# A two-layer attention trunk on one core: each pair of heads handed to the next block inside the last output-projection tile

## The chip, the cores and the metric

The kernel runs on one core of one Trainium2 chip, in fp32 throughout. The metric is device time of one execution in microseconds, here the median of three runs. The engines are named as the profile names them: PE (TensorE matmul), DVE (VectorE), ACT (ScalarE), POOL (GpSimd) and SP (SyncE, which issues nearly every DMA of this kernel).

## The reference

The input is x, 2048 tokens by 1024. Two layers follow one another, each with a residual:

```python
# layer 0
proj = rms_norm(x) @ w_in
ya = sliding_window_sink_attention(aq, ak, av, sinks) * silu(ag)   # 8 query heads of 64
yb = chunked_relbias_attention(bq, bk, bv, rel) * silu(bg)         # 8 heads of 64
x = x + concat(ya, yb) @ w_out
# layer 1
q, k, v, gate = split(rms_norm(x) @ w_in)
a = softmax(q1 k1') - lam * softmax(q2 k2')                        # 8 heads, chunk-causal
o = rms_norm(a v) * (1 - lambda_init)
x = x + (o * silu(gate)) @ w_out
```

The product with w_out is the output projection that this case is about. Its contraction runs over 1024 columns, which are eight groups of 128: in layer 0 a group is a pair of heads of 64, in layer 1 it is one head (whose value width is 128).

## The kernel before

**Precision.** A product that must keep fp32 quality is made of three matmuls of split operands (`mm3`, L212 to L216): high times high, low times high, high times low. The split itself is two instructions: ACT copies the value to the high part, rounded, and POOL subtracts it from the original to give the low part. In layer 0 this is `split_y` (ACT L608, POOL L609, tiles yH and yL), in layer 1 `split` (ACT L997, POOL L998, both tiles called cy).

**Tiling.** The 2048 tokens are four blocks of 512 (`NB`, `BLK`), each of four rows of 128 (`NTB`). The output projection of a block is eight tiles of 128 tokens by 512 columns. A tile takes `KT` = 8 steps, one for each group of 128 contracted columns, of three matmuls each, and ends in an add of the residual on DVE (L501, L1077) and a store. In layer 0 the tiles of a block are done by `projected` through `out_tile`, in layer 1 by `projected` through `out_begin`, `out_step` and `out_end`. A residual tile of layer 1 (xr) and the tiles that hold a fetched head share one pool tag, "ot", with four buffers. The split y of layer 1 takes 16 buffers, which one block fills, so a head of the next block gets its pair only when the last tile of the block before has read that head.

**Two streams, woven.** In both layers `pace` draws from a stream of attention work (`heads`, and behind it the values of each head, lagging by LAG0 or LAG1 units) and a side stream. The side stream's units are the steps of gates and output projections. `pace` lets the side advance to `share(u)`, where u is the attention work done in units; a step that yields 1 counts, whether it issues matmuls or not. In layer 0 the share is 0.85 u; in layer 1 it runs on straight lines through `STAGES1`, of which the last goes from 84 side units at u = 44 to 520 at u = 1088, which is the end of the attention work. Layer 1's side has 4 x 8 x 9 = 288 units of gates, 3 x 8 x 9 = 216 of output tiles of blocks 0 to 2, and 16 of fetches. Side matmuls carry `issue_after(self.anchor)`: they are queued on PE behind the latest score matmul. A scheduler then sets the final order on each engine; each engine runs its own queue in order.

**Between two blocks.** In layer 0 the next block's eight `split_y` are eight side units of their own ahead of its first tile. `heads` also forces the side on (`next(side)`, not counted) when the y tiles of two blocks would not fit. In layer 1 finished heads mostly wait in DRAM (`s["o"]`). `fetch(b)` reads them back one by one (DMA L1008, tile coy) and splits them, one side unit each. Block 0's heads and five of block 3's are split in place and never fetched.

**Attention of layer 1.** For each row of 128 queries, the scores (PE L898, L899) go into four PSUM banks; DVE takes the maximum (L902), ACT the exponential (L905). At the end of a row DVE joins the chunks' sums (L914 to L917: L914 multiplies two 128x8 SBUF tiles). POOL then scales both maps (L921, L930) and adds them (L931); every fifth chunk DVE makes that addition itself (L928). Later PE transposes the probabilities (L944), ACT or DVE copies them out of PSUM (L947, L949), and PE multiplies by the values (L951). At the end of a head POOL multiplies by the gate (L972).

Of the kernel before, what the change touches and what calls it, by code (L numbers as in the profile page):

```python
# [85 lines left out]
class Trunk:  # L86
# [3 lines left out]
    FIN = 18  # L90
    COMB = 5
    BANKS1, LAG1 = (4, 2, 1, 1), (30, 30, 36, 36)
    STAGES1 = ((0, 0), (44, 84), (1088, 520))

    def __init__(self, ctx, tc, args, out):
        self.ctx, self.tc, self.nc = ctx, tc, tc.nc
# [389 lines left out]

    def out_tile(self, y, w, j, t, c, xin, xout, sb, pmm, n, tag, xtag="xr", xbufs=None):
        nc = self.nc  # L490
        tok, cs = slice(t * P, (t + 1) * P), slice(c * 512, (c + 1) * 512)
        xr = sb.tile([P, 512], F32, tag=xtag, name=n + "xr", bufs=xbufs)
        nc.sync.dma_start(xr, xin[tok, cs])
        ps = pmm.tile([P, 512], F32, tag=tag, name=n + "om")
        for k in range(KT):
            self.mm3(
                ps, y[k][0][:, j * P:(j + 1) * P], y[k][1][:, j * P:(j + 1) * P],
                w[0][k][c], w[1][k][c], k == 0, k == KT - 1, self.anchor,
            )
            yield 1  # L500
        nc.vector.tensor_tensor(xr, ps, xr, ALU.add)  # L501
        nc.sync.dma_start(xout[tok, cs], xr)
        yield 1
# [16 lines left out]
    def _mix0(self, es):  # L520
# [84 lines left out]
        def split_y(yt):  # L605
            yH = yp.tile([P, BLK], F32R, tag="yH", name=n + "yH")
            yL = yp.tile([P, BLK], F32R, tag="yL", name=n + "yL")
            nc.scalar.activation(yH, yt, AF.Copy)  # L608
            nc.gpsimd.tensor_tensor(yL, yt, f32(yH), ALU.subtract)  # L609
            return yH, yL  # L610
# [134 lines left out]
                ys[4 + h // 2] = finish(yt, 512 + (h // 2) * P, b)  # L745

        units = [(j, c) for c in range(2) for j in range(NTB)]
        split = [[] for _ in range(NB)]

        def projected(b):  # L750
            for k in range(KT):
                split[b].append(split_y(done[b][k]))
                yield 1
            for j, c in units:
                while next_load(c):
                    pass
                pm, tag = (pO, "O") if b == 0 and j % 2 else (pmm, "om")
                yield from self.out_tile(split[b], w, j, b * NTB + j, c, a["x"], self.x1, yp, pm, n, tag, xbufs=2)

        def late_gate(b, c, wg, h, r0):  # L760
            cs = slice(c * P, (c + 1) * P)
# [80 lines left out]
    def _mix1(self, es):  # L842
# [155 lines left out]
            nc.gpsimd.tensor_tensor(yL, o, f32(yH), ALU.subtract)  # L998
            y[b][h] = yH, yL

        def fetch(b):

            for h in range(8):
                while (h, b) not in ended:
                    yield 0
                if h not in y[b]:
                    o = ot.tile([P, BLK], F32, tag="ot", name=n + "oy")
                    nc.sync.dma_start(o, s["o"][h * P:(h + 1) * P, b * BLK:(b + 1) * BLK])  # L1008
                    split(h, b, o)
                    yield 1  # L1010

        def load_k(h, i, m):

# [66 lines left out]
        def projected(b):  # L1080

            halves = (1, 0) if b % 2 else (0, 1)
            w = [(room[0][:, k, :], room[1][:, k, :]) for k in range(KT)]
            for i, c in enumerate(halves):
                for j in range(NTB):
                    xr, ps, to = out_begin(b, j, c)
                    for k in range(KT):
                        out_step(b, j, k, ps, w)
                        if i == 0 and j == NTB - 1:
                            load_w(halves[1], k, w[k])  # L1090
                        yield 1
                    out_end(xr, ps, to)
                    yield 1
# [72 lines left out]
        def side():  # L1166
            yield from gates()
            for b in range(NB):
                yield from fetch(b)
                yield from projected(b) if b < NB - 1 else projected_last()  # L1170

        def share(u):
# [47 lines left out]
```

## Time and profile before

| what | value |
| --- | --- |
| median of three runs | 2870.75 us (2856.9 to 2872.15) |
| the profiled execution's own time | 2868.88 us |
| its span, first to last instruction | 2867.1 us |
| mean granted TensorE clock | 0.982 |
| PE busy | 2717.2 us |
| DVE busy | 1856.3 us |
| POOL busy | 1595.3 us |
| ACT busy | 1544.8 us |

The profile is of one execution. In a timeline row the first number is the start in microseconds from the start of the span, the second the duration of the merged instructions, then engine, source line, operation, `out<-in`, and the count; brackets give the idle time of the engine ahead of it and what ended it. In a row of windows each engine's busy time in that stretch is given in the order PE, PEld (weight load), DVE, ACT, POOL, then the granted TensorE clock as a share of full speed, the DMA engines' busy share and GB/s.

### The profile page before, as it was taken

What the parts mean: (1) busy time and instruction counts of PE and PEld (TensorE: products, weight loads), DVE (VectorE), ACT (ScalarE), POOL (GpSimd) and SP (SyncE); (2) the same over time, 40 slices, a digit from 0 to 9 for tenths busy, and PEclk for the clock granted to TensorE, in tenths of its full rate; (3) what the DMA queues carried; (4) which work ended last, traced back from release to release, by engine and by line L of the source; (5) the groups of instructions that cost most, each with busy time, mean ns of one, the idle gap of its engine ahead of it and who ended that gap; (6) DMA issues with size and microseconds to landing.
All of it is one profiled execution on the core that took longest, in us unless ns stands there. A gap on an engine that the chain in (4) does not pass through costs nothing.

```text
span 2867.1 us, 43943 instructions
## 1 busy us (share of the span) xinstructions
PE 2717.2 (95%) x13384; PEld 2177.3 (76%) x13384; DVE 1856.3 (65%) x4643; ACT 1544.8 (54%) x4015; POOL 1595.3 (56%) x1740
## 2 busy tenths in 40 slices
PE   7999999998899999899999998999999999899999
PEld 5888888787788888777788887776667777566666
DVE  7752285357788875598708860477777677766761
ACT  4443543367767665343344331577777776656652
POOL 3541251334545354267745650578878787878772
PEclk9999999999999999999999999999999999999999
DMA  5673343738877664567875443887858667354543
GB/s 160 226 239 140 114 142 116 232 107 226 229 188 194 181 180 144 191 219 238 264 245 170 132 145 104 268 244 202 235 171 232 180 199 206 112 171 141 149 137 108
DMA packets 356092, 521.68 MB, mean 182 GB/s; under 512 B 44816, under 2 KB 139792, under 8 KB 355856
## 3 DMA queue, kind: packets, MB, share of 16 engines
q1 hardware_dynamic: 355856, 518.87, 60.5%
q8 instruction: 107, 1.75, 0.3%
q14 instruction: 129, 1.06, 0.1%
HBM read 361.70 MB, written 157.02 MB: 181 GB/s over the span
## 4 chain that ended last, share of the span: by engine, by line
PE 71%; DVE 8%; DMA 7%; ACT 4%; issue 2%; POOL 2%; SPq 1%; DVEq 0%; ACTq 0%; POOLq 0%
PE cO L951 7%; PE p1mm L216 5%; PE p1mm L215 5%; PE p1mm L214 5%; PE cS L898 4%; PE cS L899 4%; PE ctr L944 3%; PE p0mm L214 2%; PE p0mm L216 2%; PE p0mm L215 2%; PE com L214 2%; PE com L215 2%; PE com L216 2%; PE mom L214 2%; PE mom L215 2%
## 5 line engine op out<-in xcount | busy, mean ns | idle before, releaser
L905 ACT ACTIVATE cP<-cS,cnm 128x512 f32<-128x512 f32 (+3 forms) x640 | 397.6, 628 | 191.5 <-DVE cnm L902 170.8
L902 DVE TENSOR_REDUCE cnm<-cS 128x1 f32<-128x512 f32 (+3 forms) x640 | 374.3, 603 | 72.4 <-PE cS L899 65.3
L921 POOL TENSOR_SCALAR cP<-cP,crl,ce 128x512 f32<-128x512 f32 (+3 forms) x288 | 215.8, 762 | 186.9 <-DVE crl L916 99.4
L215 PE MATMUL p1mm<-p1wL,p1hH 128*128 128x512 f32 x768 | 302.3, 394 | 0.4 <-POOL p1wL L310 0.4
L214 PE MATMUL p1mm<-p1wH,p1hH 128*128 128x512 f32 x768 | 301.2, 393 | 0.8 <-ACT p1wH L308 0.8
L216 PE MATMUL p1mm<-p1wH,p1hL 128*128 128x512 f32 x768 | 301.9, 393 | 0.0
L951 PE MATMUL cO<-cpt,cv 128*128 128x512 f32 (+3 forms) x640 | 288.6, 539 | 12.3 <-DVE cpt L949 9.6
L310 POOL TENSOR_TENSOR p0wL<-p0ws,p0wH 128x512 fp32r<-128x512 f32 (+1 forms) x124 | 149.7, 1239 | 265.4 <-ACT p0wH L308 255.8
L931 POOL TENSOR_TENSOR cP<-cP,cP 128x512 f32<-128x512 f32 (+3 forms) x256 | 284.9, 1136 | 1.3
L898 PE MATMUL cS<-ck,cqd 128*128 128x512 f32 (+3 forms) x640 | 263.2, 416 | 18.9 <-ACT cP L905 12.0
L310 POOL TENSOR_TENSOR p1wL<-p1ws,p1wH 128x512 fp32r<-128x512 f32 x128 | 169.7, 1346 | 134.3 <-ACT p1wH L308 128.8
L214 PE MATMUL p0mm<-p0wH,p0hH 128*128 128x512 f32 (+1 forms) x640 | 239.1, 375 | 5.2 <-ACT p0vt L472 3.7
L216 PE MATMUL p0mm<-p0wH,p0hL 128*128 128x512 f32 (+1 forms) x640 | 239.5, 375 | 1.5 <-DVE p0hL L336 1.5
L215 PE MATMUL p0mm<-p0wL,p0hH 128*128 128x512 f32 (+1 forms) x640 | 239.1, 374 | 0.0
L899 PE MATMUL cS<-ck,cql 128*128 128x512 f32 (+3 forms) x640 | 234.0, 370 | 4.0 <-DMA cql<-qL 4.0
L944 PEld LDWEIGHTS ctr<-ident,cP 128*128 128x128 f32 x1088 | 137.6, 142 | 115.0 <-issue 60.9
L930 POOL TENSOR_SCALAR cP<-cP,crl,ce 128x512 f32<-128x512 f32 (+3 forms) x230 | 181.4, 800 | 0.7 <-DVE crl L917 0.7
L944 PE MATMUL ctr<-ident,cP 128*128 128x128 f32 x1088 | 174.7, 275 | 2.8 <-POOL cP L931 2.0
L214 PEld LDWEIGHTS p1mm<-p1wH,p1hH 128*128 128x128 f32 x768 | 144.7, 189 | 29.8 <-ACT p1wH L308 1.0
L215 PEld LDWEIGHTS p1mm<-p1wL,p1hH 128*128 128x128 f32 x768 | 144.7, 188 | 29.6 <-POOL p1wL L310 0.8
L216 PEld LDWEIGHTS p1mm<-p1wH,p1hL 128*128 128x128 f32 x768 | 144.7, 188 | 28.7
L898 PEld LDWEIGHTS cS<-ck,cqd 128*128 128x128 f32 x640 | 123.0, 193 | 49.7 <-ACT cP L905 25.6
(306 smaller groups left out, 7296.2 us busy)
## 6 DMA issues: line engine op xcount, KB each, us to landing
p1ws<-in_od_w_in_dram SPq DMA_DIRECT2D x56, 512.0 KB, 4.4
p0ws<-in_ev_w_in_dram SPq DMA_DIRECT2D x48, 512.0 KB, 4.5
ck<-kH SPq DMA_DIRECT2D x144, 128.0 KB, 3.3
ck<-kL SPq DMA_DIRECT2D x144, 128.0 KB, 3.5
cv<-v SPq DMA_DIRECT2D x72, 256.0 KB, 4.2
cqd<-qH SPq DMA_DIRECT2D x128, 128.0 KB, 4.8
cql<-qL SPq DMA_DIRECT2D x128, 128.0 KB, 4.8
cwH<-wgH SPq DMA_DIRECT2D x64, 256.0 KB, 4.6
```

The costliest lines, as they stand in the source:

```text
L214: mm(ps, aH, bH, start=first, stop=False)
L215: mm(ps, aH, bL, start=False, stop=False)
L216: mm(ps, aL, bH, start=False, stop=last)
L310: low.tensor_tensor(l[:, :width], ws[:, k, :width], f32(h[:, :width]), ALU.subtract)
L898: mm(ps, qd[:, m, js], kt[:, :wd], start=True, stop=False)
L899: self.anchor = mm(ps, ql[:, m, js], kt[:, :wd], start=False, stop=True).ins
L902: nc.vector.tensor_reduce(nm[:, m, z:z + 1], ps, AX.X, ALU.max, negate=True)
L905: nc.scalar.activation(chunks[z][:, :wd], ps, AF.Exp, bias=nm[:, m, z:z + 1], accum_out=acc)
L921: nc.gpsimd.tensor_scalar(p1, p1, rl[:, 0:1], e1, ALU.mult, ALU.mult)
L931: nc.gpsimd.tensor_tensor(p1, p1, p2, ALU.add)
L944: nc.tensor.transpose(tp[:, (j - j0) * P:(j - j0 + 1) * P], us[j][kt // 4][:, kk:kk + P], self.ident)
L951: mm(O[:, j0 * P:], v, T[:, :wd], start=(kt == 0), stop=(kt == nkt - 1), skip_group_check=True)
```

## The change

Layer 0: `out_tile` takes the order of the eight contraction steps and a function that is called behind each step. All tiles now go through the pairs in the order in which they finish (0, 4, 1, 5, 2, 6, 3, 7). In the last tile of blocks 3, 2 and 1, `follow` splits the next block's pair right behind the step that was the last to read that place. `projected` splits only what is still missing, and only such a split yields.

Layer 1: `fetch` handles one head and yields nothing. It is called behind each step of a block's last tile, and once more for what is missing ahead of the block. With the 16 fetch units gone, the end of the last stage goes from 520 to 504.

```diff
-    STAGES1 = ((0, 0), (44, 84), (1088, 520))
+    STAGES1 = ((0, 0), (44, 84), (1088, 504))
...
-        for k in range(KT):
+        for i, k in enumerate(order):
             self.mm3(
                 ps, y[k][0][:, j * P:(j + 1) * P], y[k][1][:, j * P:(j + 1) * P],
-                w[0][k][c], w[1][k][c], k == 0, k == KT - 1, self.anchor,
+                w[0][k][c], w[1][k][c], i == 0, i == KT - 1, self.anchor,
             )
+            if after:
+                after(i)
             yield 1
...
-        split = [[] for _ in range(NB)]
+        split = [{} for _ in range(NB)]
+        ended = [p + 4 * is_b for p in range(4) for is_b in range(2)]
 
         def projected(b):
-            for k in range(KT):
-                split[b].append(split_y(done[b][k]))
-                yield 1
+
+            for k in ended:
+                if k not in split[b]:
+                    split[b][k] = split_y(done[b][k])
+                    yield 1
+
+            def follow(i):
+                k = ended[i]
+                if k in done[b - 1] and len(split[b - 1]) == i:
+                    split[b - 1][k] = split_y(done[b - 1][k])
+
             for j, c in units:
...
+                after = follow if b and (j, c) == units[-1] else None
...
-        def fetch(b):
-
-            for h in range(8):
-                while (h, b) not in ended:
-                    yield 0
-                if h not in y[b]:
-                    o = ot.tile([P, BLK], F32, tag="ot", name=n + "oy")
-                    nc.sync.dma_start(o, s["o"][h * P:(h + 1) * P, b * BLK:(b + 1) * BLK])
-                    split(h, b, o)
-                    yield 1
+        def fetch(h, b):
+
+            if (h, b) in ended and h not in y[b]:
+                o = ot.tile([P, BLK], F32, tag="ot", name=n + "oy")
+                nc.sync.dma_start(o, s["o"][h * P:(h + 1) * P, b * BLK:(b + 1) * BLK])
+                split(h, b, o)
...
                     for k in range(KT):
                         out_step(b, j, k, ps, w)
-                        if i == 0 and j == NTB - 1:
+                        if j == NTB - 1 and i == 0:
                             load_w(halves[1], k, w[k])
+                        elif j == NTB - 1:
+                            fetch(k, b + 1)
                         yield 1
...
             for b in range(NB):
-                yield from fetch(b)
+                for h in range(8):
+                    while (h, b) not in ended and b < NB - 1:
+                        yield 0
+                    fetch(h, b)
                 yield from projected(b) if b < NB - 1 else projected_last()
```

In the changed file the lines of layer 0's mixing stand up to 15 lower, those of layer 1's attention 15 lower (L898 is L913, L931 is L946, L998 is L1013), and L1008 is L1020.

What moves, on PE, at the passage from block 0 to block 1 in layer 1. cS are scores (ck0_29673 and, after, ck0_29642 are the keys of one and the same head, the next one), com an output tile, cy its split head, cO values. Before:

```order
L898 MATMUL cS_30001<-ck0_29673,cqd_29544 128x512
L899 MATMUL cS_30001<-ck0_29673,cql_29545 128x512
L898 MATMUL cS_30021<-ck0_29684,cqd_29544 128x512
L899 MATMUL cS_30021<-ck0_29684,cql_29545 128x512
L214 MATMUL com_29898<-p1hH_18099,cy_29691 128x512
L215 MATMUL com_29898<-p1hL_18100,cy_29691 128x512
L898 MATMUL cS_30027<-ck0_29701,cqd_29544 128x512
L899 MATMUL cS_30027<-ck0_29701,cql_29545 128x512
L898 MATMUL cS_30044<-ck0_29713,cqd_29544 128x256
L899 MATMUL cS_30044<-ck0_29713,cql_29545 128x256
L216 MATMUL com_29898<-p1hH_18099,cy_29692 128x512
```

After, from that head's first score on:

```order
L913 MATMUL cS_29767<-ck0_29642,cqd_29512 128x512
L914 MATMUL cS_29767<-ck0_29642,cql_29513 128x512
L214 MATMUL com_29694<-p1hH_18099,cy_22676 128x512
L215 MATMUL com_29694<-p1hL_18100,cy_22676 128x512
L216 MATMUL com_29694<-p1hH_18099,cy_22677 128x512
L214 MATMUL com_29694<-p1hH_18099,cy_23173 128x512
L215 MATMUL com_29694<-p1hL_18100,cy_23173 128x512
L216 MATMUL com_29694<-p1hH_18099,cy_23174 128x512
L214 MATMUL com_29694<-p1hH_18099,cy_23676 128x512
L966 MATMUL cO_29197<-cpt_29535,cv_29116 128x384
L959 MATMUL ctr_29569<-ident_88,cP0_29111 128x128
L215 MATMUL com_29694<-p1hL_18100,cy_23676 128x512
```

Before, 79 rows without an output step lie ahead of the first com row shown, which belongs to block 1. After, eighteen matmuls of block 0's last tile stand between the first and the second piece of that head's scores (the first eight of them are shown), and block 1's first com row comes 33 rows behind the last.

POOL at the same place: L931 adds two maps, L972 multiplies by the gate, L998 makes the low part of a fetched head. Before:

```order
L972 TENSOR_TENSOR cot<-cot,cgg 128x512
L998 TENSOR_TENSOR cy<-coy,cy 128x512
L931 TENSOR_TENSOR cP_29671<-cP_29671,cP_29722 128x512
L931 TENSOR_TENSOR cP_29682<-cP_29682,cP_29737 128x512
L931 TENSOR_TENSOR cP_29699<-cP_29699,cP_29746 128x512
L998 TENSOR_TENSOR cy<-coy,cy 128x512
L931 TENSOR_TENSOR cP_29711<-cP_29711,cP_29762 128x512
L998 TENSOR_TENSOR cy<-coy,cy 128x512
L921 TENSOR_SCALAR cP_29797<-cP_29797,crl,ce 128x512
```

After:

```order
L946 TENSOR_TENSOR cP_29640<-cP_29640,cP_29687 128x512
L946 TENSOR_TENSOR cP_29651<-cP_29651,cP_29708 128x512
L946 TENSOR_TENSOR cP_29662<-cP_29662,cP_29717 128x512
L946 TENSOR_TENSOR cP_29676<-cP_29676,cP_29727 128x512
L987 TENSOR_TENSOR cot<-cot,cgg 128x512
L1013 TENSOR_TENSOR cy<-coy,cy 128x512 x2
L936 TENSOR_SCALAR cP_29771<-cP_29771,crl,ce 128x512
L1013 TENSOR_TENSOR cy<-coy,cy 128x512
```

Eight operations with two tensor inputs in a row become seven, and the four additions of the maps come ahead of the fetched heads.

SP at the same place: coy is a fetch, cgg a gate, cv values, cxr a residual tile in, out_0_dram a finished tile out. Before, behind three fetches that stand among the next head's query loads:

```order
L964 DMA cgg_30787<-g1_75 128x512
L1008 DMA coy_29808<-o1_76 128x512
L1008 DMA coy_29822<-o1_76 128x512
L1008 DMA coy_29846<-o1_76 128x512
L1024 DMA cv_30269<-v_74 128x4x128
L1008 DMA coy_29860<-o1_76 128x512
L1008 DMA coy_29874<-o1_76 128x512
L1067 DMA cxr_29896<-x1_83 128x512
```

After, behind all of those query loads:

```order
L1020 DMA coy_29698<-o1_76 128x512
L1020 DMA coy_29735<-o1_76 128x512
L1089 DMA out_0_dram<-cxr_29692 128x512
L1020 DMA coy_29785<-o1_76 128x512
L979 DMA cgg_30773<-g1_75 128x512
L1020 DMA coy_29802<-o1_76 128x512
L1020 DMA coy_29829<-o1_76 128x512
L1020 DMA coy_29854<-o1_76 128x512
L1035 DMA cv_30260<-v_74 128x4x128
L1020 DMA coy_29871<-o1_76 128x512
L1020 DMA coy_29888<-o1_76 128x512
L1078 DMA cxr_29923<-x1_83 128x512
```

The fetches no longer stand among the query loads, two of them stand ahead of the last tile's store, and two loads of values and the next keys still stand behind all eight.

More of the change, by code (lines that the diff above doesn't have):

```diff
@@ L757, in projected @@
                 pm, tag = (pO, "O") if b == 0 and j % 2 else (pmm, "om")
-                yield from self.out_tile(split[b], w, j, b * NTB + j, c, a["x"], self.x1, yp, pm, n, tag, xbufs=2)
+                after = follow if b and (j, c) == units[-1] else None
+                yield from self.out_tile(
+                    split[b], w, j, b * NTB + j, c, a["x"], self.x1, yp, pm, n, tag, xbufs=2, order=ended, after=after
+                )
         def late_gate(b, c, wg, h, r0):
```

2 lines of the change are left out of this document (1 added, 1 removed).

## The prediction

> **What bounds the kernel now.** I read the page first, then the busy time in stretches of 50 us, then the timeline of each engine where a stretch falls short.
>
> ```profile
> span 2867.1 us, 43943 instructions
> PE 2717.2 (95%) x13384; PEld 2177.3 (76%) x13384; DVE 1856.3 (65%) x4643; ACT 1544.8 (54%) x4015; POOL 1595.3 (56%) x1740
> ...
> 2250.00:2300.00 50.00, 49.89 (x229) 36.14 (x228) 35.39 (x90) 36.62 (x103) 38.16 (x45) 1.00 0.55 165
> 2450.00:2500.00 50.00, 38.54 (x156) 24.73 (x156) 38.12 (x66) 30.47 (x83) 44.54 (x47) 0.86 0.46 131
> 2650.00:2700.00 50.00, 45.88 (x194) 32.74 (x192) 35.73 (x62) 31.68 (x86) 42.78 (x45) 0.93 0.49 143
> ```
>
> PE is the bound: 150 us of the span are all that it leaves idle. Where side steps are spread evenly (2250 to 2300) nothing is left. The worst stretch of layer 1's attention, 11.5 us idle at a clock of 0.86, is the passage from block 0 to block 1; the passage from block 1 to 2 lies at the head of the last one. On PE at the first:
>
> ```profile
> 2473.57 0.50 PE L214 MATMUL com<-p1hH,cy 128*128 128x512 f32 x1 [0.99 <-ACT cy L997]
> 2477.66 0.50 PE L216 MATMUL com<-p1hH,cy 128*128 128x512 f32 x1 [2.46 <-POOL cy L998]
> 2486.76 2.08 PE L951 MATMUL cO<-cpt,cv 128*128 128x512 f32 x2 [7.18 <-DVE cpt L949]
> ...
> 2485.00:2490.00 5.00, 3.24 (x7) 1.92 (x8) 2.29 (x8) 0.27 (x1) 4.21 (x6) 0.50 0.22 57
> 2490.00:2495.00 5.00, 5.00 (x16) 2.72 (x15) 1.18 (x2) 3.02 (x6) 4.57 (x5) 0.83 0.00 0
> ```
>
> Two waits are for the first fetched head, the third is for DVE. Then the clock costs 3.24 x 0.50 + 5.00 x 0.17 = 2.5 us. The passage loses 0.99 + 2.46 + 7.18 + 2.5 = 13.1 us. What held DVE stands in its own rows and POOL's:
>
> ```profile
> 2468.74 0.16 DVE L916 RECIPROCAL crl<-cl 128x2 f32<-128x2 f32 x1
> 2475.61 9.35 DVE L914 TENSOR_TENSOR cpe<-ce,cla 128x8 f32<-128x8 f32 x1
> 2674.77 0.17 DVE L914 TENSOR_TENSOR cpe<-ce,cla 128x8 f32<-128x8 f32 x1 [0.27 <-ACT ce L913]
> ...
> 2469.10 3.04 POOL L921 TENSOR_SCALAR cP<-cP,crl,ce 128x512 f32<-128x512 f32 x4 [0.75 <-ACT cP L905]
> 2472.11 3.04 POOL L930 TENSOR_SCALAR cP<-cP,crl,ce 128x512 f32<-128x512 f32 x4
> 2475.10 1.28 POOL L972 TENSOR_TENSOR cot<-cot,cgg 128x512 f32<-128x512 f32 x1
> 2483.66 1.28 POOL L998 TENSOR_TENSOR cy<-coy,cy 128x512 fp32r<-128x512 f32 x1
> ```
>
> L914 takes 0.17 us elsewhere. Here it started 0.5 us into POOL's run of eight operations on two tensors (the first and the last of them are shown) and ended when the run did, 9.35 us later. While L914 stood, DVE's copies out of PSUM stood behind it, and PE's value matmuls behind those. The Trainium skill says the same of the cause: "GPSIMD Engine Reference", section Specifications, has GpSimd share its SBUF interfaces with VectorE, with contention for DVE instructions that have two SBUF inputs. It gives no price, and this trace's is the 9.35 us. It speaks against this change, which takes no such operation off POOL; what follows from that is the second rival.
>
> **The change part by part.** No matmul, split or DMA is added or taken away. What goes is eight side units without a matmul at each passage; so eight steps come forward into the time where PE had no side work.
>
> *Layer 1, block 0 to 1.* A run of side steps on PE:
>
> ```profile
> 2836.04 0.39 PE L214 MATMUL com<-p1hH,cyk 128*128 128x512 f32 x1
> 2841.26 0.39 PE L216 MATMUL com<-p1hH,cyk 128*128 128x512 f32 x1
> ```
>
> They are the first and the last of 24, so one costs 5.22 / 23 = 0.227 us and eight steps 5.4 us. POOL starts a row of the attention when DVE's L916 is done (2468.9), spends 6.1 us on eight scalings, and is then on its run; the next L914 came 6.7 us after that L916 and was caught at once. After the change eighteen matmuls of the last tile, 4.1 us, stand inside that row, so L914 comes after some 10.8 us. The run is now seven operations of about 1.23 us and lies from 6.1 to 14.7, so 3.9 us of it are left for L914 to wait out. At PE's share of before (7.18 of 9.35) that leaves 3.0 us idle, a gap like those under 3 us, of which I take no loss of clock. The two waits for the first head I halve to 1.7: it is fetched a tile earlier, but its low part stands at the end of the same POOL run. Gain 13.1 - 4.7 = 8.4 us, between 0 (L914 is caught as before) and 13.1.
>
> *Layer 1, block 1 to 2.*
>
> ```profile
> 2638.19 0.50 PE L898 MATMUL cS<-ck,cqd 128*128 128x512 f32 x1 [0.75 <-ACT cP L905]
> 2641.45 0.39 PE L898 MATMUL cS<-ck,cqd 128*128 128x256 f32 x1 [0.98 <-DVE cnm L902]
> 2642.64 0.50 PE L214 MATMUL com<-p1hH,cy 128*128 128x512 f32 x1 [0.68 <-ACT cy L997]
> 2648.90 0.66 PE L944 MATMUL ctr<-ident,cP 128*128 128x128 f32 x4 [0.65 <-ACT csq L977]
> 2673.33 0.80 PE L898 MATMUL cS<-ck,cqd 128*128 128x512 f32 x1 [3.17 <-ACT cP L905]
> ...
> 2663.93 7.88 DVE L928 SCALAR_TENSOR_TENSOR cP<-cP,cc,cP 128x256 f32<-128x256 f32 x1
> ...
> 2664.07 3.75 POOL L998 TENSOR_TENSOR cy<-coy,cy 128x512 fp32r<-128x512 f32 x3
> 2667.79 3.73 POOL L931 TENSOR_TENSOR cP<-cP,cP 128x512 f32<-128x512 f32 x3
> ...
> 2670.00:2675.00 5.00, 1.83 (x5) 1.38 (x5) 4.62 (x9) 2.50 (x8) 1.52 (x2) 0.76 0.21 70
> 2675.00:2680.00 5.00, 5.00 (x13) 3.32 (x13) 2.63 (x8) 3.13 (x9) 4.46 (x7) 0.55 0.30 92
> ```
>
> Idle 6.2 us, clock 1.83 x 0.24 + 5.00 x 0.45 = 2.7 us, together 8.9. Again a run on POOL, three splits and three additions, held a DVE operation. In the new order POOL has two splits, three additions (one a quarter long) and three splits in a row here, a longer run. So I take half of the first four gaps (1.5) and a quarter of the last with its clock (1.5): 3.0 us, between 0 and 8.9.
>
> *Layer 1, block 2 to 3.* The three fetches now stand in the last tile instead of behind the last head. I cost it at nothing: block 3's first three heads are in place, and their steps cover the fetch; without that cover it would cost the two waits of the first passage, 3.5 us.
>
> *Layer 0.* The order of steps changes no count. Of the passages, block 3 to 2 and block 2 to 1 show losses:
>
> ```profile
> 906.36 0.63 PE L736 MATMUL mtrB<-ident,mPB 128*128 128x128 f32 x4 [0.91 <-DVE mptL L589]
> 908.06 1.12 PE L736 MATMUL mtrB<-ident,mPB 128*128 128x128 f32 x4 [1.07 <-DVE mptL L589]
> 913.66 0.44 PE L736 MATMUL mtrB<-ident,mPB 128*128 128x128 f32 x2 [0.78 <-DVE mptL L589]
> 915.06 0.33 PE L736 MATMUL mtrB<-ident,mPB 128*128 128x128 f32 x1 [0.71 <-DVE mptL L589]
> 1053.63 0.39 PE L582 MATMUL mSB<-mks,mqd 128*128 128x256 f32 x1 [1.57 <-DVE manm L633]
> ...
> 905.00:910.00 5.00, 3.02 (x19) 2.62 (x17) 4.90 (x11) 2.49 (x7) 5.00 (x6) 0.79 1.11 292
> 910.00:915.00 5.00, 3.47 (x20) 2.70 (x18) 3.65 (x10) 4.28 (x14) 3.82 (x7) 0.86 0.99 224
> 1055.00:1060.00 5.00, 5.00 (x23) 4.43 (x22) 2.64 (x12) 3.21 (x13) 1.21 (x3) 0.69 0.25 70
> ```
>
> The first loses 3.5 idle and 3.02 x 0.21 + 3.47 x 0.14 = 1.1 of clock, 4.6 us; the second 1.6 and 5.00 x 0.31 = 1.6, 3.1 us. Counting the yields, `heads` forces the side on by twelve units at one point of the second; after the change it forces none. Eight steps, 5.4 us, fit both holes. I take 3.5 and 2.0, between 0 and 7.7. Block 1 to 0 lies behind the attention, where the order stays but for the splits: nothing.
>
> *What it adds.* First, a block's first tile now follows the last one directly, and its first matmul may wait for DVE to free the only bank:
>
> ```profile
> PE com L214 <- DVE cxr L1077: 5.4, 4, 2.1
> ```
>
> That is 1.35 us a time, 2.7 for two passages (0 to 4.2). Second, layer 1's side runs at 420 instead of 436 units over the same stretch, 3.7% slower. From u = 44 to about 240, where PE isn't yet full, three steps come later: 9 x 0.227 = 2.0 us, of which I take 1.5 (0 to 2.0). Third, ACT's split of a next head waits for the step that last read its place; behind it stand exponentials. PE waited for ACT's fetched split 0.99 us at worst in the rows above, and I count it in the halved waits.
>
> Sum: 8.4 + 3.0 + 3.5 + 2.0 = 16.9; less 2.7 + 1.5 = 4.2; 12.7 us. The profiled execution took 2868.88 us, 1.9 less than the median of 2870.75. 2868.88 - 12.7 gives **2856 us**. One sentence on the clock: "TensorE: Matmul & The Clock Gate" of the Trainium skill, section Why this matters for your kernels, warns of PE gaps over about 3 us, and the trace agrees at 7.18 and 3.17 us.
>
> **The rivals.** *All stalls go.* If no DVE operation meets a POOL run at a passage, all of 13.1 + 8.9 + 7.7 = 29.7 us come back, less 2.0: 2841 us. For it: stretches with even side work have no idle time. Against: the new order still has runs of seven and more.
>
> *The stalls move.* POOL's two-tensor operations are as many as before, and runs of 7, 6 and 8 still stand at the passages. If L914 or L928 is caught as before, layer 1 gains nothing: 2868.9 - 5.5 + 4.2 = 2868 us, no change. For it: the 9.35 and 7.88 us were caught by chance of timing, so others can be.
>
> *SP is held (slower).* A fetch needs one of four "ot" buffers, and the last tile's residual now holds one while the fetches queue:
>
> ```profile
> 2801.95 12.26 SPq L1008 DMA_DIRECT2D coy<-o  x3
> ```
>
> Three fetches held SP for 12.3 us there. In the new order values and the next keys stand behind eight. If SP is held that long at both passages and the loads land 12 us late with 3 us of lead, PE waits 9 us twice and loses 2.5 us of clock twice; with layer 1's gains gone: 2868.9 + 23 - 5.5 + 4.2 = 2891 us. It decides once SP stands longer than the loads' lead. Against: the next head's queries now stand ahead of the fetches, and the passage shown held SP without holding PE.
>
> **How the numbers follow.** My forecast, stalls shortened, has 0.61; all stalls gone 0.11; stalls moved 0.16; SP held 0.12. The measurement can tell 0.5%, 14.4 us, from no change: below 2856.4 is faster. The forecast lies on that line, so half of it (0.31) is faster and half the same. Faster 0.31 + 0.11 = 0.42, same 0.30 + 0.16 = 0.46, slower 0.12. The forecast's own bounds are 2868.9 - 29.7 + 2.0 = 2841 and about 2869. The range leaves out the slow case and a few us more for reordered queues everywhere in layer 1 on both sides: 2836 to 2875.
>
> **What would show it.** Right: side steps on PE through both passages, L914 there under 5 us, idle at the first passage under 6 us, the clock in 50 us there over 0.95. Wrong: a DVE operation of 8 us or more beside a run of POOL (stalls moved), an SP row of fetches over 10 us with PE waiting for ck, cv or cqd (SP held), or new idle time of over 5 us outside the passages, which no term here holds.

## The result, and the profile after

The changed kernel takes 2841.76 us (median of 6 runs, 2832.64 to 2846.43) against 2870.43 us before (6 runs, 2856.9 to 2876.98). The ratio is 0.9901 with a 95% interval of 0.9878 to 0.9923: 28.7 us faster, between 22 and 35. The forecast of 2856 us has the sign right and half of the size; the range of 2836 to 2875 us holds the result.

The page of the changed kernel, span and PE's row:

```profile
span 2841.6 us, 43911 instructions
PE 2707.3 (95%) x13384; PEld 2171.4 (76%) x13384; DVE 1844.8 (65%) x4643; ACT 1543.8 (54%) x4015; POOL 1596.6 (56%) x1740
```

The span is 25.5 us shorter. The work on PE is the same 13384 matmuls, so both executions can be cut at the same points of the work: the bounds are the moments at which 8800, 10600, 11800, 12200 matmuls and so on have started on PE. The busy time in these stretches, of the kernel before and then of the changed one (columns: stretch, its length, then busy time and instructions of PE, PEld, DVE, ACT and POOL, the granted clock, DMA share, GB/s):

```profile
0.00:1793.57 1793.57, 1695.69 (x8800) 1428.80 (x8801) 1135.71 (x2883) 859.13 (x2099) 806.53 (x850) 0.99 0.60 181
1793.57:2207.05 413.48, 393.52 (x1802) 294.30 (x1800) 294.12 (x823) 287.27 (x830) 307.41 (x364) 0.98 0.79 228
2207.05:2471.18 264.13, 261.74 (x1203) 191.72 (x1201) 193.71 (x466) 187.52 (x528) 212.00 (x238) 1.00 0.62 181
2471.18:2580.81 109.63, 95.40 (x400) 66.31 (x401) 73.43 (x135) 62.54 (x168) 85.08 (x93) 0.92 0.51 151
```

```profile
0.00:1792.22 1792.22, 1694.97 (x8800) 1428.92 (x8801) 1138.23 (x2883) 859.85 (x2099) 804.95 (x850) 0.99 0.61 181
1792.22:2194.16 401.94, 387.06 (x1802) 289.42 (x1801) 295.61 (x835) 289.92 (x843) 310.79 (x368) 1.00 0.81 233
2194.16:2459.55 265.39, 263.29 (x1201) 192.28 (x1200) 198.61 (x451) 182.35 (x514) 216.06 (x242) 1.00 0.63 183
2459.55:2554.13 94.58, 92.15 (x402) 65.35 (x401) 63.98 (x145) 65.39 (x177) 81.94 (x87) 0.96 0.56 176
```

Read the lengths against each other. Up to layer 1's attention 1.4 us are gained; in the second row, where the gates are computed and no passage lies, 11.5; then 1.3 are lost; and 15.1 are gained in the row of the first passage. What follows is in the table below: 4.6 us more up to the last stretch, and 5.8 given back there. 1.4 + 11.5 - 1.3 + 15.1 + 4.6 - 5.8 = 25.5 us.

**The first passage.** The timelines of SP, DVE, PE and POOL of the changed kernel there, then its busy time in 5 us:

```profile
2451.24 0.17 DVE L931 RECIPROCAL crl<-cl 128x2 f32<-128x2 f32 x1
2457.11 0.50 SPq L1078 DMA_DIRECT2D cxr<-x  x1
2462.41 0.69 DVE L1088 TENSOR_TENSOR cxr<-com,cxr 128x512 f32<-128x512 f32 x1 [2.27 <-DMA coy<-o]
2463.76 2.07 PE L966 MATMUL cO<-cpt,cv 128*128 128x512 f32 x2 [2.13 <-DVE cpt L964]
2465.69 1.27 POOL L1013 TENSOR_TENSOR cy<-coy,cy 128x512 fp32r<-128x512 f32 x1 [0.66 <-ACT cy L1012]
2467.53 0.17 DVE L929 TENSOR_TENSOR cpe<-ce,cla 128x8 f32<-128x8 f32 x1 [2.32 <-ACT ce L928]
```

```profile
2455.00:2460.00 5.00, 4.54 (x23) 3.07 (x21) 3.58 (x7) 3.31 (x10) 5.00 (x6) 1.00 0.91 179
2460.00:2465.00 5.00, 2.65 (x6) 1.32 (x7) 2.72 (x7) 2.99 (x11) 5.00 (x5) 0.78 0.66 220
2465.00:2470.00 5.00, 5.00 (x11) 2.39 (x10) 0.70 (x5) 2.21 (x7) 2.92 (x4) 0.54 0.66 205
```

The operation that stood 9.35 us on DVE (L914, now L929) takes 0.17 us, and the wait of 7.18 us behind it is gone. It came late enough: 16.3 us behind the row's L931 (L916 before), and 0.6 us after POOL's run of two-tensor operations had ended with the row of L1013 shown. What is left is 2.8 us idle and, with the clock, 2.65 x 0.22 + 5.00 x 0.46 = 2.9 us. It has a new reason: SP issues the last tile's residual, "cxr", only at 2457.1, behind the keys and queries; DVE stands for it at L1088 until 2462.4 (the row names the fetch that SP issued next, which L1088 does not read; the residual landed at 2462.39), its copies out of PSUM stand behind, and PE's value matmuls behind those. The second passage looks alike, in the timelines and in 5 us:

```profile
2617.09 0.69 DVE L1088 TENSOR_TENSOR cxr<-com,cxr 128x512 f32<-128x512 f32 x1 [2.87 <-DMA cxr<-x]
2620.39 1.27 SPq L1020 DMA_DIRECT2D coy<-o  x3
2624.77 0.63 ACT L1012 ACTIVATE cy<-coy 128x512 fp32r<-128x512 f32 x1 [4.09 <-DMA coy<-o]
2625.45 0.50 PE L214 MATMUL com<-p1hH,cy 128*128 128x512 f32 x1 [2.75 <-ACT cy L1012]
```

```profile
2620.00:2625.00 5.00, 2.71 (x14) 1.69 (x13) 3.83 (x10) 0.91 (x3) 4.40 (x6) 1.00 0.67 179
2625.00:2630.00 5.00, 4.54 (x13) 3.28 (x14) 2.35 (x4) 5.00 (x14) 5.00 (x6) 0.66 0.35 115
```

DVE stands 2.87 us for the residual, ACT 4.09 us for a fetched head to land (SP issued it at 2620.39, when the last tile's store had landed at 2620.38 and freed an "ot" buffer), and PE 2.75 us for ACT's split of it: 2.29 + 0.46 us idle and 4.54 x 0.34 = 1.5 us of clock, 4.3 together.

**The end.** PE's timeline behind the last head in the changed kernel, its busy time there, and PE's one wait at that place in the kernel before:

```profile
2806.61 1.12 PE L991 MATMUL cms<-csq,ones 128*128 128x512 f32 x2 [1.35 <-ACT csq L983]
2811.41 0.79 PE L214 MATMUL com<-p1hH,cyk 128*128 128x512 f32 x1 [3.67 <-ACT cyk L1012]
```

```profile
2810.00:2815.00 5.00, 3.59 (x10) 2.89 (x11) 0.69 (x1) 0.63 (x1) 1.28 (x1) 0.66 0.16 52
```

```profile
2826.89 1.13 PE L976 MATMUL cms<-csq,ones 128*128 128x512 f32 x2 [1.35 <-ACT csq L968]
```

Before, side steps were left when the last head was done, and they covered its norm and split. Now they are used up: PE waits 3.67 us more and loses 3.59 x 0.34 = 1.2 us of clock. The change moved work forward out of a place where it was cover.

**The gates' stretch.** Three windows of 10 us in which the kernel before loses and the changed one does not, its timelines in one of them, and the windows of the changed kernel for the same work:

```profile
2110.00:2120.00 10.00, 7.66 (x28) 4.64 (x27) 7.93 (x14) 7.01 (x20) 5.66 (x6) 0.83 0.47 133
2130.00:2140.00 10.00, 6.53 (x30) 4.94 (x28) 8.64 (x13) 4.60 (x16) 8.70 (x10) 1.00 0.72 224
2140.00:2150.00 10.00, 9.84 (x35) 7.20 (x36) 6.15 (x19) 6.98 (x20) 5.60 (x9) 0.83 0.41 122
```

```profile
2133.11 5.12 DVE L914 TENSOR_TENSOR cpe<-ce,cla 128x6 f32<-128x6 f32 x1
2139.22 0.50 PE L898 MATMUL cS<-ck,cqd 128*128 128x512 f32 x1 [3.43 <-ACT cP L905]
```

```profile
2110.00:2120.00 10.00, 10.00 (x51) 7.98 (x50) 7.49 (x20) 7.26 (x22) 10.00 (x12) 1.00 0.85 197
2120.00:2130.00 10.00, 9.70 (x42) 6.74 (x41) 9.04 (x23) 7.37 (x25) 8.44 (x10) 1.00 0.81 256
2130.00:2140.00 10.00, 10.00 (x48) 7.22 (x47) 9.34 (x17) 7.73 (x20) 9.38 (x12) 1.00 0.34 102
```

From 2110 to 2150 the kernel before lost 2.3 + 3.5 + 0.2 us idle and 1.3 + 1.7 us of clock, 9.0 together; now 0.3 is lost. A product on DVE that stood 5.12 us, and PE's wait for ACT's exponential behind it, are part of it. From 2010 to 2020 the kernel before loses 5.7 us more, in and behind a wait of 5.05 us for a gate's weights; the changed kernel has such a wait as well, of 3.05 us. No passage is near: all that the change does here is to pace the gates by 504 instead of 520.

### The profile page after: what moved, and what is told of

Read it like the earlier page. It is cut to its first block, busy times and chain, and to the rows that moved or that the text cites. A ratio compares the mean times of both kernels' runs of the same rounds, so it can differ in the third digit from the quotient of the medians.

```text
span 2841.6 us, 43911 instructions
## 1 busy us (share of the span) xinstructions
PE 2707.3 (95%) x13384; PEld 2171.4 (76%) x13384; DVE 1844.8 (65%) x4643; ACT 1543.8 (54%) x4015; POOL 1596.6 (56%) x1740
## 4 chain that ended last, share of the span: by engine, by line
PE 73%; DVE 9%; DMA 9%; ACT 4%; issue 2%; POOL 2%; SPq 1%; DVEq 0%; ACTq 0%; POOLq 0%
PE cO L966 7%; PE p1mm L214 5%; PE p1mm L216 5%; PE p1mm L215 5%; PE cS L913 4%; PE cS L914 4%; PE ctr L959 3%; PE p0mm L214 3%; PE p0mm L216 3%; PE p0mm L215 3%; PE com L214 2%; PE com L215 2%; PE com L216 2%; PE mom L214 2%; PE cG L214 2%
## 5 line engine op out<-in xcount | busy, mean ns | idle before, releaser
L946 POOL TENSOR_TENSOR cP<-cP,cP 128x512 f32<-128x512 f32 (+3 forms) x256 | 285.5, 1140 | 1.4
L913 PE MATMUL cS<-ck,cqd 128*128 128x512 f32 (+3 forms) x640 | 261.2, 413 | 12.4 <-ACT cP L920 7.1
L914 PE MATMUL cS<-ck,cql 128*128 128x512 f32 (+3 forms) x640 | 231.4, 367 | 4.4 <-DMA cql<-qL 4.4
L913 PEld LDWEIGHTS cS<-ck,cqd 128*128 128x128 f32 x640 | 121.9, 191 | 44.6 <-ACT cP L920 19.9
```

The lines of the kernel that those rows point to most:

```text
L913: mm(ps, qd[:, m, js], kt[:, :wd], start=True, stop=False)
L914: self.anchor = mm(ps, ql[:, m, js], kt[:, :wd], start=False, stop=True).ins
L946: nc.gpsimd.tensor_tensor(p1, p1, p2, ALU.add)
```

## The experiments

Each kernel's stretches, cut at the same counts of matmuls (us, each from one profiled execution). "Passage 1" is the 11800th to the 12200th, the column behind it goes on to the 13200th and holds the second passage, "end" goes to the 13380th. "Pace" is the last number of STAGES1. On the chip of the three kernels with one run the kernel before takes 2862.28 us.

| kernel | pace | to layer 1's attention | gates | up to passage 1 | passage 1 | passage 2 and on | end | ratio to before |
|---|---|---|---|---|---|---|---|---|
| before | 520 | 1793.6 | 413.5 | 264.1 | 109.6 | 238.9 | 42.6 | 1 |
| e1, layer 0 alone | 520 | 1779.3 | 410.3 | 263.6 | 108.6 | 238.1 | 42.6 | 0.9983 (0.9967 to 0.9999) |
| e5, split on DVE | 520 | 1785.9 | 416.7 | 264.2 | 98.7 | 234.1 | 42.6 | 0.9954 (0.9936 to 0.9972) |
| e10 | 512 | 1791.3 | 417.1 | 271.2 | 108.8 | 233.2 | 42.6 | one run, 2870.77 us |
| e4, pace alone | 504 | 1789.4 | 401.0 | 265.7 | 97.3 | 244.8 | 44.2 | 0.9950 (0.9933 to 0.9966) |
| e11 | 488 | 1792.2 | 402.7 | 275.5 | 105.9 | 245.1 | 41.9 | one run, 2869.86 us |
| changed | 504 | 1792.2 | 401.9 | 265.4 | 94.6 | 234.4 | 48.4 | 0.9901 (0.9878 to 0.9923) |
| e2, layer 1 alone | 504 | 1788.2 | 400.6 | 265.5 | 92.5 | 234.1 | 48.6 | 0.9901 (0.9884 to 0.9918) |
| e3, gates as at 520 | 504 | 1787.7 | 408.6 | 275.2 | 95.4 | 228.9 | 49.6 | 0.9943 (0.9924 to 0.9961) |
| e6, changed, split on DVE | 504 | 1788.1 | 405.8 | 264.6 | 95.3 | 234.0 | 48.9 | 0.9944 (0.9924 to 0.9965) |
| e9, changed, 8 units left | 496 | 1785.8 | 402.5 | 266.5 | 92.5 | 237.9 | 42.6 | 0.9880 (0.9860 to 0.9899) |
| e7, changed | 496 | 1784.2 | 409.9 | 265.4 | 104.2 | 236.2 | 42.6 | 0.9945 (0.9927 to 0.9964) |
| e12, changed | 488 | 1791.6 | 400.3 | 274.6 | 95.5 | 238.3 | 44.1 | one run, 2850.95 us |

How far such a row can be trusted shows in pairs with one and the same layer 1: before and e1 run the same matmuls in the same order there and agree within 3.2 us, changed and e2 likewise within 2.1. Layer 0 does not repeat so: e1 and the changed kernel have the same layer 0 and took 1779.3 and 1792.2 us up to layer 1's attention.

**e1: layer 0 alone.** Its edit:

```diff
-            for k in range(KT):
-                split[b].append(split_y(done[b][k]))
-                yield 1
+            for k in ended:
+                if k not in split[b]:
+                    split[b][k] = split_y(done[b][k])
+                    yield 1
...
+                after = follow if b and (j, c) == units[-1] else None
```

> The kernel before with the change in layer 0 alone (order of steps by ended, splits in the last tile's steps); layer 1 and its pace as before. The prediction priced this part at 5.5 us of gain; the two traces, laid beside each other by the count of PE's matmuls, show 1.9 us at the layer's end. Theory A (layer 0 is worth what the traces show): 1 to 2 us faster, ratio about 0.9995. Theory B (the prediction's size): 5.5 us faster, 0.998. Both can hardly be told apart by the time alone; the lag at PE's 8800th matmul tells (1.9 against 5.5 us).

Measured 0.9983, 4.9 us, with an interval from 0.3 to 9.5. It holds both sizes, and one trace can't decide, since layer 0 differs by 13 us between two profiles of the same code. All profiles together: the seven kernels with the new layer 0 reach layer 1's attention after 1787.0 us on average, the six with the old one after 1790.1. These 3.1 us lie between the two sizes, and the spread of the single profiles, 8 and 13 us, leaves both open. That layer 1 alone (e2) reaches the ratio of the whole change fits the smaller one, within intervals of 5 to 6 us to either side.

**e2: layer 1 alone, with the pace of 504.** Its edit is the diff without out_tile and layer 0.

> The kernel before with the change in layer 1 alone, its pace end of 504 included; layer 0 as before. Theory A (all but 2 us of the gain comes from layer 1): 26 to 27 us faster, ratio 0.9907. Theory B (layer 0's order bears a part through what it hands on): under 20 us faster, 0.993 or more.

0.9901, the same ratio as of the whole change, as theory A has it.

**e3: the changed kernel with the gates paced as before.**

```diff
-    STAGES1 = ((0, 0), (44, 84), (1088, 504))
+    STAGES1 = ((0, 0), (44, 84), (532, 288), (1088, 504))
```

> The changed kernel, but the gates are paced as before (84 to 288 side units from u = 44 to 532), and only the output steps follow the new end of 504. The traces show 13 us of the gain between 1850 and 2170 us, where only the gates' pace differs; the prediction had a loss of 1.5 us there. Theory A (the slower gates bring these 13 us): they are gone, 15 us faster than before, ratio 0.9945. Theory B (it is chance which DVE operation meets a run of POOL, and the profiled run of before had a bad draw): the stretch comes out anywhere between the two, about 22 us faster, 0.992. Theory C (the prediction: slower gates cost 1.5 us): 30 us faster, 0.9895.

0.9943, the ratio of theory A, but not all by its way: the gates' stretch is back at 408.6 us, 6.7 more than in the changed kernel and not 13, and DVE's L929 stands 5.10 us in it as L914 did before. Another 10 us are lost ahead of the first passage, where theory A has nothing.

**e4: the kernel before with the pace of 504.**

```diff
-    STAGES1 = ((0, 0), (44, 84), (1088, 520))
+    STAGES1 = ((0, 0), (44, 84), (1088, 504))
```

> The kernel before with the pace end 504 instead of 520 and nothing else. Theory A (slower gates bring 13 us): 13 us faster in the stretch from 1850 to 2170 us, the passages lose as before, ratio 0.9955 or a little more, since the last 16 units come late. Theory B (chance of meetings): within 6 us either way, 0.998 to 1.002. Theory C (the prediction): 1.5 us slower for the gates, and up to 3.6 us for 16 units that come after the attention, 1.001 to 1.002.

0.9950, 14.3 us faster: half of the gain comes from one number. The gates' stretch takes 401.0 us as in the changed kernel. Beyond the expectation, the first passage gained too, 12 us: DVE's L914 stood 3.88 us there, not 9.35. The second passage lost more than before, 244.8 us in its column against 238.9: L914 stood 7.78 us there, and PE 6.47 us behind it:

```profile
2486.43 3.88 DVE L914 TENSOR_TENSOR cpe<-ce,cla 128x8 f32<-128x8 f32 x1
2660.20 7.78 DVE L914 TENSOR_TENSOR cpe<-ce,cla 128x8 f32<-128x8 f32 x1 [1.64 <-ACT ce L913]
```

With the pace equal at 504, the fetch within the last tile itself is worth e2 against e4, on one chip: 2838.71 to 2851.11 us, 12.4 us. In the table it gives 4.8 us at the first passage and 10.7 in the column of the second, which e4 had drawn badly, and takes 4.4 back at the end.

**e5 and e6: split's subtraction on DVE,** in the kernel before and in the changed one.

```diff
-            nc.gpsimd.tensor_tensor(yL, o, f32(yH), ALU.subtract)
+            nc.vector.tensor_tensor(yL, o, f32(yH), ALU.subtract)
```

> The kernel before, with the subtraction of split (the low part of a gated head, 32 of them) moved from POOL to DVE; all else as before. It breaks the runs of two-tensor operations on POOL at the passages, and leaves the side steps where they were. Theory A (a DVE operation on two SBUF tensors is held until POOL's run ends): DVE L914 at the first passage no longer stands 9.35 us, and L928 at the second not 7.88; PE's gaps of 7.18 and 3.17 us go, with about 3 us of clock; 32 x 0.7 us more on DVE lie beside PE. About 10 to 13 us faster, ratio 0.996. Theory B (the passages lose because PE has no side steps there, and the held operation is only what PE happens to wait for): the gaps stay, with another releaser; within 4 us, 0.9985 to 1.001.

0.9954, theory A. DVE's L914 at the first passage and L928 at the second, with POOL's run and the wait that PE is left with:

```profile
2470.83 0.28 DVE L914 TENSOR_TENSOR cpe<-ce,cla 128x8 f32<-128x8 f32 x1
2649.02 0.99 DVE L928 SCALAR_TENSOR_TENSOR cP<-cP,cc,cP 128x256 f32<-128x256 f32 x1
2472.29 3.41 POOL L931 TENSOR_TENSOR cP<-cP,cP 128x512 f32<-128x512 f32 x2
2472.94 0.50 PE L216 MATMUL com<-p1hH,cy 128*128 128x512 f32 x1 [1.56 <-DVE cy L998]
```

The holds of 9.35 and 7.88 us are gone, and the passage takes 98.7 us, 10.9 less than before and 4.1 more than in the changed kernel. The hole in the side steps ahead of it is as long as before: 21.1 us without an output matmul, where the kernel before has 21.5. So the passage lost most of its time to the held operation, and the missing side steps cost little. The parting is not clean: with the split on DVE fourteen output matmuls of block 1 stand ahead of the value matmuls that had waited, where five stood before. Nine matmuls are 9 x 0.227 = 2.0 us, and the wait for the first head's low part is 0.9 us shorter.

> The changed kernel with the same move of split's subtraction to DVE. The passages of the changed kernel still lose 5.3 and 5.2 us (idle and clock), the first behind DVE's copy and reduction, the second behind ACT's split, none behind a held DVE operation of over 4 us. Theory A (the lock is what is left there): 5 us faster than the changed kernel, 0.988 against before. Theory B (what is left is ACT's and the bank's): no change against the changed kernel, 0.990 against before.

0.9944 with its interval from 0.9924, where the changed kernel's ends at 0.9923: by the ratios 12 us slower than it, by the medians 5, which neither theory had. The two ran on different chips and their intervals all but touch, so the loss itself is not settled. The profiled span is the changed kernel's own, 2841.6 us, and the stretches differ by 4.1 us at most; the passage did not gain, which speaks for theory B.

**e7, e10, e11, e12: other paces.** e7 and e12 edit the changed kernel, e10 and e11 the kernel before:

```diff
-    STAGES1 = ((0, 0), (44, 84), (1088, 504))
+    STAGES1 = ((0, 0), (44, 84), (1088, 496))
```

> The changed kernel with the pace end 496 instead of 504: the gates 1.9% slower again, and 8 side units left when the attention is paced out. Theory A (a slower gate pace is what saves the 13 us between 1850 and 2170): that stretch gains as much or more, and 8 steps, 1.8 us, fill the end, where the changed kernel loses 6 us behind the last head: 2 to 6 us faster than it, 0.988 to 0.9895 against before. Theory B (the pace draws which DVE operation meets a run of POOL, and 504 drew well): part of the 13 us comes back, 0.991 to 0.995.

0.9945, theory B: the gates' stretch is back at 409.9 us, and the first passage takes 9.6 us more than in the changed kernel.

> The kernel before with the pace end 512 instead of 520, one look. The stretch from PE's 8800th to its 10600th matmul, in which the gates are computed, took 413.4 us at 520 and 401.4 at 504, with the rest of the kernel the same; the changed kernel took 402.4 at 504 and 410.4 at 496. Theory A (slower gates are better, up to a point between 504 and 496): between 404 and 410 here. Theory B (a draw: each pace has its own meetings of DVE operations and POOL runs): anything from 399 to 418, with no order by pace.

417.1 us, against theory A. Half of what PE stands idle there is no matter of DVE and POOL: 13.0 of 25.8 us are waits for the gates' weights (6.6 us before, 7.3 in the changed kernel), more than half of them at one place:

```profile
2008.61 0.80 PE L214 MATMUL cG<-p1hH,cwH 128*128 128x512 f32 x1 [7.40 <-DMA cwH<-wgH]
```

> The kernel before with the pace end 488, one look. Theory A (an optimum near 504): the stretch from PE's 8800th to its 10600th matmul takes 412 us or more. Theory B (a draw): anything from 399 to 418. The passages have the steps where they were, but at other points of the attention: the first passage's wait behind a DVE operation of over 4 us may or may not be there.

402.7 us: theory A has fallen here. The stretch is short although DVE's products were held in it again, one of them for 4.27 us:

```profile
2117.32 4.27 DVE L914 TENSOR_TENSOR cpe<-ce,cla 128x6 f32<-128x6 f32 x1
```

> The changed kernel with the pace end 488, one look. Theory A (an optimum near 504): the stretch of the gates takes 412 us or more, and the whole is slower than the changed kernel by 8 us or more. Theory B (a draw): the stretch as in the kernel before at 488, within 3 us, whatever that is, since up to there the two differ only in layer 0.

400.3 us, within 2.4 us of e11, as theory B asks. Its one run is 11 us under the median of the kernel before on its chip, where the changed kernel is 28.7 under on its own; 9 us of the difference are lost between the gates and the first passage. By pace the gates' stretch took 409 to 417 (520, with e3), 417 (512), 401 to 406 (504, with e9), 410 (496) and 400 to 403 us (488). It has no order from pace to pace. So the pace is the cause, by e4, but how it acts is shown in single places only: a held product in the kernel before, the gates' weights in e10. And 504 was a lucky number: of the four paces of the kernel before, it alone is clearly faster; e10 and e11 took no less than the kernel before in their one run each. The first passage, against that, took 92 to 96 us in six of the seven kernels that fetch within the last tile, 104.2 in e7 only, and 97 to 110 in the five that fetch behind it with the split on POOL.

**e8: the hold by itself.** None of the trunk is computed.

```python
nc.gpsimd.tensor_tensor(g, A, B, ALU.add)            # n times, 128x512
nc.scalar.activation(C[:, :8], g[:, :8], AF.Copy)    # after the first of them
nc.vector.tensor_tensor(v[:, :8], C[:, :8], e8, ALU.mult)
```

> None of the trunk is computed: a measurement of the lock by itself. POOL runs n operations on 128x512 back to back, of two SBUF tensors (T) or of one tensor and two per-row numbers (S); the end of the first lets ACT copy 128x8, and that releases one DVE operation: a product of two 128x8 SBUF tensors (TT8), a 128x8 tensor by a per-row number (TS8), a reduction of 128x8 (TR8), a sum of two 128x512 (TT), a scaled sum (STT), a sum with a PSUM operand (PT), a copy (PC) and a reduction (PR) out of PSUM. Theory A (held until the run ends): TT8 takes 0.2 us beside S of five and about 4 us beside T of five, 0.5 to 1 beside T of two, 2 beside three and about 9 beside nine; TT and STT are held too; TS8, TR8, PC and PR are not, or far less. Theory B (the two share the port in turn, and no run matters): TT8 takes at most one POOL operation, 1.3 us, whatever the run's length.

Runs on POOL and single operations on DVE (vTT of 128x8 is TT8, vTS is TS8, vSTT is STT, vPT is PT):

```profile
8.59 0.97 DVE L58 TENSOR_TENSOR vTT<-tC,te 128x8 f32<-128x8 f32 x1 [1.78 <-ACT tC L86]
90.72 6.13 POOL L81 TENSOR_TENSOR gT<-tA,tB 128x512 f32<-128x512 f32 x5
92.26 4.62 DVE L58 TENSOR_TENSOR vTT<-tC,te 128x8 f32<-128x8 f32 x1 [3.71 <-ACT tC L86]
98.46 0.49 DVE L58 TENSOR_TENSOR vTT<-tC,te 128x8 f32<-128x8 f32 x1 [1.30 <-ACT tC L86]
102.83 4.63 DVE L60 TENSOR_SCALAR vTS<-tC,ts 128x8 f32<-128x8 f32 x1 [3.14 <-ACT tC L86]
135.26 1.49 DVE L66 SCALAR_TENSOR_TENSOR vSTT<-tC,ts,tA 128x512 f32<-128x512 f32 x1 [3.14 <-ACT tC L86]
146.27 0.69 DVE L68 TENSOR_TENSOR vPT<-tQ,tA 128x512 f32<-128x512 f32 x1 [3.11 <-ACT tQ L86]
182.36 11.01 POOL L81 TENSOR_TENSOR gT<-tA,tB 128x512 f32<-128x512 f32 x9
183.90 0.97 DVE L58 TENSOR_TENSOR vTT<-tC,te 128x8 f32<-128x8 f32 x1 [2.85 <-ACT tC L86]
```

The hold is real: a product of 128x8 takes 4.62 us, to the end of POOL's run of five, and 0.49 us beside scalings. An operation by a per-row number in SBUF is held as well (4.63 us), against what I expected; one with an operand in PSUM is not (0.69 us). Its length is not settled. Each trial ran twice, and the product beside five, entered at the same point of the run's second operation, took 0.97 us the first time and 4.62 the second. Beside the run of nine it was let through after 0.97 us both times, at the end of one POOL operation, and so was the scaled sum beside five (1.49 us). Theory A holds in some trials and B in others; what decides between them was not found. "SBUF — State Buffer" of the Trainium skill, section SBUF: two separate sides, makes the shared ports a lock that is held for a whole instruction, by whoever starts first, while the other blocks. The 0.97 us agree; the 4.62 us are four POOL instructions, and the trunk's 9.35 us eight, which the page's rule does not give. The 4.63 us of the per-row product fit another page of the Trainium skill, "VectorE: DVE Perf Modes", section Mode 2×_2P — use both read ports for one tensor: there an fp32 product with a scalar reads one tensor through both ports, so it needs the shared one too.

**e9: the changed kernel with 8 side units left for the end.**

```diff
-    STAGES1 = ((0, 0), (44, 84), (1088, 504))
+    STAGES1 = ((0, 0), (44, 84), (930, 440.4), (1088, 496))
```

> The changed kernel with the same pace up to u = 930 (behind the passage from block 1 to 2) and then 8 side units fewer up to the end of the attention: 496 instead of 504. So 8 output steps are left when the last head is normalized, where the changed kernel waits 1.35 and 3.67 us and loses 1.2 us of clock. Theory A (the waits come from the side having run out): 24 matmuls, 5.4 us, fill them; the wait of com for ACT's cyk is under 1 us, 4 to 5 us faster than the changed kernel, ratio 0.9885 against before. Theory B (the new order of the last block's passage costs as much): no change against the changed kernel, 0.990.

0.9880, 2827.56 us against 2862.28 on that chip. PE's only row with a wait behind the last head, and the busy time around it:

```profile
2792.38 1.13 PE L991 MATMUL cms<-csq,ones 128*128 128x512 f32 x2 [1.35 <-ACT csq L983]
```

```profile
2790.00:2795.00 5.00, 3.65 (x16) 2.35 (x15) 1.03 (x2) 3.20 (x6) 2.60 (x3) 1.00 0.00 0
2795.00:2800.00 5.00, 5.00 (x24) 4.16 (x23) 1.42 (x2) 1.54 (x3) 4.58 (x3) 1.00 0.50 172
```

The wait of 3.67 us and the low clock are gone, and the end takes 42.6 us instead of 48.4: theory A. In time it is the fastest kernel of all; its interval overlaps that of the changed kernel, so the 5.8 us rest on the trace.

## Why the prediction was right, and where it was off

*The total: partly luck.* 12.7 us were forecast, 28.7 measured. Without the gates, 14.2 us were forecast (12.7 + 1.5) and the columns give 14.0 (25.5 - 11.5), but by errors that cancel: the first passage gave 6.7 us more than its term, layer 0 4.1 less, and the end took 5.8 that no term held.

*Block 0 to 1: the hold was read rightly, the rest not.* 8.4 us were forecast. L929 takes 0.17 us, better than the 3.9 us that I left it: it came 16.3 us into the row instead of 10.8, with the output steps and the wait for the residual ahead of it. The passage still loses 5.7 us where I left 4.7, by that other wait: the residual's load, which I had only as a held "ot" buffer. In stretches the first passage gained 15.1 us, since the hold of 3.79 us on L928 at 2537.90, which I left out of the sum, went too. e5 supports that the hold was the main cause. But the hold is a matter of which operation meets which run, and e4 shows that the pace alone brings 12 of the 15 us here.

*Block 1 to 2.* 3.0 forecast, 4.6 measured in its column, and 10.7 at equal pace (e2 against e4). *Block 2 to 3:* nothing forecast, and no row contradicts it.

*Gates' pace: the step that failed.* "Layer 1's side runs at 420 instead of 436 units over the same stretch" was priced at a loss of 1.5 us, by the matmuls that come later. It gained 11.5. I counted the matmuls that a slower pace withholds, and not that another pace deals all meetings of the engines and the loads anew, in a stretch where the kernel before lost 9 us within 40. I had a part of the reason in hand: the second rival says that the held operations "were caught by chance of timing", and I wrote that L914 takes 0.17 us elsewhere, while it stood 5.12 us in this very stretch. I applied the holds to the passages only.

*The end: a term that the sum lacked.* The eight steps that came forward at each passage were priced as gain only. At the end they had been cover; 4.9 us of wait and clock came in their place, and e9 gives most of it back.

*Layer 0.* 5.5 us forecast, 1.4 by the two traces, 3.1 by the average of all, 0.3 to 9.5 by the runs. The passage from block 3 to 2 improved, from 4.6 us to 1.4; that from block 2 to 1 did not, since another wait stands there now, as the busy time and PE's timeline of the changed kernel show:

```profile
905.00:915.00 10.00, 8.55 (x53) 6.96 (x53) 7.44 (x24) 7.03 (x24) 5.80 (x10) 1.00 0.94 246
```

```profile
1046.62 0.69 PE L739 MATMUL mtrB<-ident,mPB 128*128 128x128 f32 x2 [2.56 <-DVE mptL L592]
```

*Waits of com for cxr:* 2.7 us of new ones were forecast. None came: PE waits so 3.6 us in two places, where it waited 5.4 in four. DVE's own waits for the residual stand in their place, inside the passages' remainders.

*The rivals.* "All stalls go" names the measured time, 2841 us, and is wrong: the passages still lose 5.7 and 4.3 us and the end 6.2, and 11.5 us come from a stretch that it doesn't speak of. "The stalls move" is wrong for the first passage (92 to 96 us in six of seven kernels) and right in e7. "SP is held" occurs in small: DVE stood 2.27 and 2.87 us for a residual that SP issued late, and at the second passage SP waited for an "ot" buffer with the third fetch. PE lost 2.13 us at the first passage and 2.75 at the second by it, not 9.

*The signs that I named.* Side steps on PE through both passages: no, at the first none stands between 2455.0 and 2470.2. L914 under 5 us: yes. Idle at the first passage under 6 us: yes, 2.8. The clock in 50 us there over 0.95: no, 0.93, after the wait of 2.13 us:

```profile
2450.00:2500.00 50.00, 47.19 (x199) 32.01 (x198) 31.91 (x73) 34.79 (x95) 46.55 (x50) 0.93 0.50 145
```

What stays open: what one pace loses and another does not could not be told ahead of the run, and is traced in single places only; what ends a hold; and layer 0's share.

## What to carry to other kernels

A number that only sets the pace of a weave is a change to every meeting of engines behind it: here 520 to 504 was worth 14 us by itself and 496 in the changed kernel took 12 us back, so give it its own run before you credit the code that came with it, and don't carry the number over. When steps are moved forward to fill a hole, ask what they covered where they were. A short DVE operation with a long time in the trace is read against POOL's row at the same moment; moving POOL's part of the work away, as e5 did, tests it in one line, once you have looked at what else the move reorders.

## What the runs showed of the hardware

A DVE operation of 0.17 us on SBUF tensors stood up to 9.35 us beside back-to-back POOL operations on two tensors. It was held by itself too (4.62 us beside five, 0.97 in the same trial's other turn), with a per-row operand as well (4.63), and not with an operand in PSUM (0.69). POOL pays as well: with DVE's two-tensor subtractions beside it, two additions took 3.41 us (e5), where three took 3.73 in the kernel before while DVE was held. In the trunk the long holds repeat with the program's order: before and e1, with the same layer 1, have DVE held 9.35 and 9.27 us at the first passage, 5.12 and 5.10 in the gates' stretch.
